# Alternating full and half-width experts, and wider weight blocks, in a mixture-of-experts layer

## The chip, the cores and the metric

The kernel runs on one core of a Trainium2 chip. The metric is device time in microseconds of one execution. Three executions of the kernel before gave 1993.58 us in the median (1984.93 to 1996.19). A separate execution was profiled; all rows below are from that one.

## The reference

Two transformer layers over 256 latent and 256 context tokens of width 1024, all in float32. The change concerns only the last step of the second layer, a mixture of eight experts of which each of the 256 latent tokens takes the best two:

```python
def moe_swiglu(h, w_router, wg, wu, wd):
    logits = t @ w_router
    top_v, top_i = lax.top_k(logits, 2)
    gates = ...            # softmax of the two, zero for the other experts
    for e in range(8):
        y = y + gates[:, e:e + 1] * ((silu(t @ wg[e]) * (t @ wu[e])) @ wd[e])
```

Each `wg[e]` and `wu[e]` is 1024 x 3584 and each `wd[e]` is 3584 x 1024, so an expert has 44.04 MB of weights and the eight have 352.3 MB. A token block is at most 128 rows, so every weight is used for few columns of work: weights have to stream in from HBM all through this step.

## The kernel before

The kernel runs the first layer, then the second layer's mixer, and ends with the experts, which take the second half of its time.

**Two kinds of expert.** The experts are sorted by how many tokens they got (`order_experts`, `order_index`), but for expert 0, which starts before the order is known. The first `NBIG` = 4 of them are *full*: up to 128 tokens each, handled by `expert`. The other four are *small*: up to 64 tokens, handled by `expert_small`. They run in the order 0 to 7, so all full ones come first. SP reads the order into registers in `load_order` (line 1049) and uses it in the addresses of all later weight loads. Tokens over these capacities would be handled in a loop at the end that is skipped where there are none.

**A full expert.** Weights come in loads of 1 MiB through `load_e`, each into a slot of a ring of 2048-column buffers (`slot32`; the names of the slots stand in `first` and `ring`, and `until` says up to which load a borrowed slot may be used: from load 62 on five slots are left). `convert` then splits each load in two float32r parts: ACT writes the high part `eh` (line 804), DVE subtracts to get the low part `el` (line 805). Three pairs of buffers hold converted weights. The product is made of three matmuls (high x high, high x low, low x high; `mm3`). The 3584 columns go in seven blocks of 512. For block j the order on the PE is: gate into PSUM tile `pg` (two loads, 24 matmuls of 512 columns), transposes of block j-1 (`g_T`), up into `pu` (the same again), `act_mul` (ACT: Silu of `pg`; DVE: times `pu`), and `down` of block j-1 into `pd` (two loads, 24 matmuls, line 1148). The last block's transposes and `down`, and the scatter of the result to the token rows (`scatter_pre`, `scatter_half`), are a *tail* that runs inside the first block of the next expert.

**A small expert.** The same loop without conversion: the loads are used as plain float32 (`load_raw`, line 1232), so a slot stays taken until the PE has read it. Gate and up go together into the two halves of the partitions of one PSUM tile `pgs` (line 1268); a matmul of 512 columns shows as two PE instructions, so that a block has 32 of them for gate and up, and 16 for down (`pds`, line 1256). The scatter writes `py` (line 1310).

**Loads.** All weight loads are issued by SP, in program order, one after the other; SP waits at each until its slot is free. A gate or up load takes 512 rows of 2048 contiguous bytes, a down load 256 rows of 4096 bytes. Loads that fit are issued before the experts begin: `prefetch` brings the first three while the mixer runs, and the slots of `first` are filled as soon as the mixer gives its memory back.

**Side work.** `plan` hangs small pieces of work on (expert, block): the ordering, the one-hot selections, the gathers of the token columns for later experts (`gather_at`, `gather_pair`, `gather_rest`), and broadcasts of vectors (`row_bc`).

## Time and profile before

| | |
|---|---|
| median of three executions | 1993.58 us |
| profiled execution | 1992.54 us |
| its span (first to last instruction) | 1990.6 us |
| mean granted TensorE clock | 0.979 |
| PE busy | 1851.6 us (93%) |
| DVE busy | 1000.7 us (50%) |
| ACT busy | 766.9 us (39%) |
| HBM read | 477.48 MB, 240 GB/s over the span |

PE is the engine for matmuls, DVE the vector engine, ACT the scalar engine, SP the engine that issues the loads. "Busy" sums the stretches in which an engine executed something; matmuls overlap in the pipeline, so a busy PE is not a PE at its peak. Shares over the whole span mix stages of different limits; the change touches the stage from 1006 us to the end.

### The profile page before, as it was taken

Reading aid. Unit: us, or ns where it says so; the run is one execution under the profiler, and the core shown is the slowest. Engines: PE = TensorE matmul, PEld = TensorE weight load, DVE = VectorE, ACT = ScalarE, POOL = GpSimd, SP = SyncE. Lnnn points to the kernel's source line nnn. Section 1 sums busy time; section 2 is a strip of 40 time slices with the busy share of each in tenths; the row PEclk is TensorE's granted clock in tenths of the full one; section 3 lists DMA queues with packets and bytes.
Section 4 is the critical chain, followed back from the end, with each engine's and each line's share of the span. In section 5 each row is a group of like instructions: output and inputs, shape, how many; then the busy total and the mean of one; then the engine's idle time right before and its main releaser. Section 6 shows DMA issues by size and latency. Waiting matters only on the chain.

```text
span 1990.6 us, 23382 instructions
## 1 busy us (share of the span) xinstructions
PE 1851.6 (93%) x9168; PEld 1275.5 (64%) x9168; DVE 1000.7 (50%) x1356; ACT 766.9 (39%) x991; POOL 49.1 (2%) x89
## 2 busy tenths in 40 slices
PE   7998999999999999999999999999999878887876
PEld 4866767778887877677677878878785322222222
DVE  5475665633333345756679788988984001010101
ACT  4324554422222234235566677767762000000001
POOL 1031000000000000200000000000000000000000
PEclk9999999999999999999989999999999999899998
DMA  9555242442344244553389688999998999999996
GB/s 326 178 166 144 69 142 71 138 137 69 101 130 157 78 127 151 141 141 127 124 300 361 243 325 312 342 350 365 348 339 289 390 394 388 377 390 386 388 385 258
DMA packets 287089, 480.13 MB, mean 241 GB/s; under 512 B 12206, under 2 KB 142636, under 8 KB 286972
## 3 DMA queue, kind: packets, MB, share of 16 engines
q1 hardware_dynamic: 283488, 474.32, 67.6%
q0 software_dynamic: 1232, 2.42, 1.0%
q10 hardware_dynamic: 2252, 1.83, 0.3%
q8 instruction: 74, 1.21, 0.3%
q14 instruction: 43, 0.35, 0.1%
HBM read 477.48 MB, written 1.05 MB: 240 GB/s over the span
## 4 chain that ended last, share of the span: by engine, by line
PE 78%; DMA 15%; DVE 4%; ACT 2%; issue 1%; SPq 0%; ACTq 0%; DVEq 0%
DMA e<-in_w_moe_up_dram 12%; PE pd L1148 8%; PE pgs L1268 6%; PE pds L1256 3%; PE pg L149 3%; PE pu L150 3%; PE pu L151 3%; PE pg L150 3%; PE pu L149 3%; PE pg L151 3%; PE psg L149 2%; PE psmod L229 2%; PE psg L150 2%; PE psg L151 2%; PE psu L149 2%; PE psp L149 2%
## 5 line engine op out<-in xcount | busy, mean ns | idle before, releaser
L805 DVE TENSOR_TENSOR el<-e,eh 128x2048 fp32r<-128x2048 f32 (+1 forms) x173 | 375.5, 2189 | 50.4 <-ACT eh L804 49.3
L804 ACT ACTIVATE eh<-e 128x2048 fp32r<-128x2048 f32 (+1 forms) x173 | 316.6, 1838 | 93.8 <-PE pd L1148 31.7
L1268 PE MATMUL pgs<-e,xs 128*64 128x512 f32 x896 | 247.6, 628 | 72.7 <-DMA e<-in_w_moe_up_dram 64.0
L1268 PEld LDWEIGHTS pgs<-e,xs 128*64 128x64 f32 x896 | 70.0, 142 | 235.0 <-DMA e<-in_w_moe_up_dram 105.7
L143 DVE TENSOR_TENSOR wl<-w,wh 128x2048 fp32r<-128x2048 f32 (+2 forms) x70 | 150.3, 2148 | 104.4 <-ACT wh L142 104.3
L142 ACT ACTIVATE wh<-w 128x2048 fp32r<-128x2048 f32 (+2 forms) x70 | 125.4, 1792 | 199.6 <-issue 78.3
L1277 DVE TENSOR_TENSOR eg<-eg,pgs 64x512 f32<-64x512 f32 x28 | 19.3, 690 | 360.7 <-ACT eg L1276 360.7
L1276 ACT ACTIVATE eg<-pgs 64x512 f32<-64x512 f32 x28 | 16.6, 591 | 374.1 <-PE pgs L1268 374.1
L1256 PE MATMUL pds<-e,gts 128*64 128x512 f32 x448 | 127.7, 599 | 0.2 <-DMA e<-in_w_moe_down_dram 0.2
L149 PE MATMUL psp<-hH,wh 128*128 128x512 f32 (+1 forms) x224 | 88.4, 397 | 3.4 <-ACT hH L274 3.3
L149 PE MATMUL pg<-eh,xeH 128*128 128x512 f32 x224 | 90.2, 403 | 0.6 <-ACT eh L804 0.6
L150 PE MATMUL pg<-el,xeH 128*128 128x512 f32 x224 | 89.9, 401 | 0.0
L151 PE MATMUL pg<-eh,xeL 128*128 128x512 f32 x224 | 89.2, 398 | 0.0
L149 PE MATMUL pu<-eh,xeH 128*128 128x512 f32 x224 | 89.0, 397 | 0.0
L150 PE MATMUL pu<-el,xeH 128*128 128x512 f32 x224 | 88.3, 394 | 0.7 <-DVE el L805 0.6
L149 PE MATMUL psq<-wh,hH 128*128 128x256 f32 x304 | 88.7, 292 | 0.0
L151 PE MATMUL psq<-wh,hL 128*128 128x256 f32 x304 | 88.2, 290 | 0.0
L150 PE MATMUL psq<-wl,hH 128*128 128x256 f32 x304 | 87.8, 289 | 0.0
L151 PE MATMUL pu<-eh,xeL 128*128 128x512 f32 x224 | 87.7, 392 | 0.0
L150 PE MATMUL psp<-hL,wh 128*128 128x512 f32 (+1 forms) x224 | 86.6, 387 | 0.0
L151 PE MATMUL psp<-hH,wl 128*128 128x512 f32 (+1 forms) x224 | 85.0, 380 | 0.0
L1148 PE MATMUL pd<-eh,gth 128*128 128x512 f32 x224 | 71.2, 399 | 2.7 <-ACT eh L804 2.5
(511 smaller groups left out, 3504.3 us busy)
## 6 DMA issues: line engine op xcount, KB each, us to landing
e<-in_w_moe_gate_dram SPq DMA_DIRECT2D x111, 1024.0 KB, 7.4
e<-in_w_moe_up_dram SPq DMA_DIRECT2D x111, 1024.0 KB, 7.7
e<-in_w_moe_down_dram SPq DMA_DIRECT2D x111, 1024.0 KB, 6.8
wmod<-in_w_mod_dram SPq DMA_DIRECT2D x96, 512.0 KB, 4.7
w<-in_w_in_dram SPq DMA_DIRECT2D x24, 1024.0 KB, 7.2
w<-in_w_ffn_gate_dram SPq DMA_DIRECT2D x11, 1024.0 KB, 7.5
w<-in_w_ffn_up_dram SPq DMA_DIRECT2D x11, 1024.0 KB, 5.2
w<-in_w_out_dram SPq DMA_DIRECT2D x8, 1024.0 KB, 5.2
```

The lines of the kernel that those rows point to most:

```text
L142: act(wh[:, :m], w32[:, :m], AF.Copy)
L143: tt(wl[:, :m], w32[:, :m], f32(wh[:, :m]), ALU.subtract)
L149: mm(ps, lhsT=sh, rhs=mh, start=first, stop=False)
L150: mm(ps, lhsT=sh, rhs=ml, start=False, stop=False)
L151: mm(ps, lhsT=sl, rhs=mh, start=False, stop=last)
L229: mm(ps[32 * k:32 * k + 32, :n], lhsT=Sz[:, k0 + k, :], rhs=wv[:, k, :], start=k0 == 0, stop=k0 == 4, skip_group_check=True)
L804: act(h3[:, b], w[:, b], AF.Copy)
L805: tt(l3[:, b], w[:, b], f32(h3[:, b]), ALU.subtract)
L1148: mm(pds[o], lhsT=gt[sh][:, q, :], rhs=w[mh][:, k, o * 512:(o + 1) * 512], start=a and j == 0 and q == 0, stop=z and j == NJ - 1 and q == 3)
L1256: mm(pd[0][H * o:H * o + H, :], lhsT=gt[:, q, :], rhs=w[:, k, o * 512:(o + 1) * 512], start=j == 0 and q == 0, stop=j == NJ - 1 and q == 3 ...
L1268: mm(ps[H * o:H * o + H, :], lhsT=xv[:, kk, :], rhs=ws[o][:, k, :], start=kk == 0, stop=kk == KD - 1, skip_group_check=True)
L1277: tt(g[0:H], g[0:H], ps[H:P], ALU.mult)
```

## The change

**Order.** The experts run as 0, 4, 1, 5, 2, 6, 3, 7: full and small ones alternate. `plan` is now keyed by place in that order and by half blocks (even keys run inside a block, odd ones behind it). The small experts' gather moves into the first full expert; the gathers for the full experts 1, 2 and 3 move into small ones.

**Blocks.** The 3584 columns go in four blocks of 896 (`FB`) instead of seven of 512. A gate or up load is 256 rows of 896 columns, 3584 contiguous bytes each and 0.92 MB in all; there are 32 per expert instead of 28. A down block of 896 rows is given to the partitions in sevens (row p*7+k goes to partition p), so a load of two k is 8192 contiguous bytes per partition; each block has three such loads of 1.05 MB and one of half that size, 16 per expert instead of 14.

**What follows from that.** Gate and up matmuls have 448 columns, two for each k in two PSUM banks; `pg` and `pu` are two banks wide and have one buffer instead of two. `act_mul` writes its result in permuted order (steps of 512 bytes within runs of seven) so that the transposes fit the new row order of down. `eg`, `gth` and `gtl` have one buffer instead of two.

**Ring.** The slot `xc` and its pieces of 1024 bytes are gone; 12 slots instead of 13 are filled first; `xl` stays in the ring to the end, so that six slots are left from load 42 on.

```diff
+FB = 896
+FK = FB // 128
...
+        m = kk * n
+        nc.sync.dma_start(w32[:, :m].rearrange("p (k n) -> p k n", n=n), dram)
+        for a in range(0, m, m // 2 if i < 8 else m):
+            b = slice(a, a + (m // 2 if i < 8 else m))
+            act(wh[:, b], w32[:, b], AF.Copy)
+            tt(wl[:, b], w32[:, b], f32(wh[:, b]), ALU.subtract)
...
+        ready[i] = convert(i, ring_tile(f"r{i}"), wm_g[0, 0, i * 256:(i + 1) * 256, 0:FB].rearrange("(k p) n -> p k n", p=P), 2, FB, mpr)
...
-    pgu = pool("pgu", 2, space=PSUM)
+    pgu = pool("pgu", 1, space=PSUM)
...
-    first = ["r0", "r1", "r2", "w", "c", "r0", "r1", "xh", "xl", "xt", "y", "r2", "xc"]
-    ring = ["w", "c", "r0", "r1", "xh", "xl", "xt", "y", "r2", "xc"]
-    until = {"xc": 36, "xt": 42, "y": 42, "xh": 62, "xl": 62}
+             "y": lambda: mp2.tile([P, 2048], F32, tag="y", name="e32")}
+    first = ["r0", "r1", "r2", "w", "c", "r0", "r1", "xh", "xl", "xt", "y", "r2"]
+    ring = ["w", "c", "r0", "r1", "xh", "xl", "xt", "y", "r2"]
+    until = {"xt": 42, "y": 42, "xh": 30}
...
-        xs = mp.tile([P, KD, n], F32, tag="xeH1", name="xs")
+        xs = mp.tile([P, KD, n], F32, tag="xeH0", name="xs")
...
+    NJ = FE // FB
+    HB = FB // 2
+
+    def gu_ap(w_ap, j, c):
+        return w_ap[c * 256:(c + 1) * 256, j * FB:(j + 1) * FB].rearrange("(k p) n -> p k n", p=P)
+
+    def down_aps(w_ap, j):
+        w = w_ap[j * FB:(j + 1) * FB, :].rearrange("(p k) n -> p k n", k=FK)
+        return [(k, min(2, FK - k), w[:, k:min(k + 2, FK), :]) for k in range(0, FK, 2)]
...
     def gate_up(w_ap, xe, j, tag):
...
+        ps = pgu.tile([P, 2, 512], F32, tag=tag, name=tag)
+        for c in range(KD // 2):
+            w = load_e(gu_ap(w_ap, j, c), 2, FB)
+            for k in range(2):
+                kk = 2 * c + k
+                for (sh, mh) in ((0, 0), (0, 1), (1, 0)):
+                    for b in range(2):
+                        mm(ps[:, b, 0:HB], lhsT=xe[sh][:, kk, :], rhs=w[mh][:, k, b * HB:(b + 1) * HB],
+                           start=kk == 0 and sh == mh, stop=kk == KD - 1 and sh == 1)
...
+    def by_row(ap):
+        return ap.rearrange("p h (q k) -> p h q k", k=FK)
+
+    def act_mul(g, pg, pu):
+        gv = g.rearrange("p (k h q) -> p h q k", h=2, q=P // 2)
+        act(gv, by_row(pg), AF.Silu)
+        tt(gv, gv, by_row(pu), ALU.mult)
+
+    def new_g():
+        return mp2.tile([P, FB], F32, tag="eg", name="eg")
 
...
+        gh = mp2.tile([P, FK, P], F32R, tag="gth", name="gth")
+        gl = mp2.tile([P, FK, P], F32R, tag="gtl", name="gtl")
+        for k0 in range(0, FK, 4):
+            n = min(4, FK - k0)
+            pt = bank(pmt, "pgt")
+            for q in range(n):
+                nc.tensor.transpose(pt[:, q * P:(q + 1) * P], g[:, (k0 + q) * P:(k0 + q + 1) * P], ident)
+            pv = pt[:, 0:n * P].rearrange("p (q n) -> p q n", n=P)
+            act(gh[:, k0:k0 + n], pv, AF.Copy)
+            tt(gl[:, k0:k0 + n], pv, f32(gh[:, k0:k0 + n]), ALU.subtract)
...
+        for q0, kn, ap in down_aps(w_ap, j):
+            w = load_e(ap, kn, D)
+            for k in range(kn):
+                q = q0 + k
...
-                           start=a and j == 0 and q == 0, stop=z and j == NJ - 1 and q == 3)
...
+                           start=a and j == 0 and q == 0, stop=z and j == NJ - 1 and q == FK - 1)
...
+            for f in (hooks or {}).get(2 * j, ()):
+                f()
             pu = gate_up(wu, xe, j, "pu")
-            g = act_mul(pg, pu)
+            g = new_g()
+            act_mul(g, pg[:, :, 0:HB], pu[:, :, 0:HB])
...
-            for f in (hooks or {}).get(j, ()):
+            for f in (hooks or {}).get(2 * j + 1, ()):
...
+            ps = pgu.tile([P, 2, 512], F32, tag=("pg", "pu")[j % 2], name="pgs")
+            for c in range(KD // 2):
+                ws = [load_raw(gu_ap(w_ap, j, c), 2, FB) for w_ap in (wg, wu)]
+                for k in range(2):
+                    kk = 2 * c + k
+                    for b in range(2):
+                        for o in range(2):
+                            mm(ps[H * o:H * o + H, b, 0:HB], lhsT=xv[:, kk, :], rhs=ws[o][:, k, b * HB:(b + 1) * HB],
...
+                if c == 1:
...
+            g = new_g()
+            act_mul(g[0:H], ps[0:H, :, 0:HB], ps[H:P, :, 0:HB])
...
-        xg = mp.tile([P, 2, D], F32, tag="xeH0", name="xg")
+        xg = mp.tile([P, 2, D], F32, tag="xeH1", name="xg")
...
-        xes[2] = gather_at(2, 2, xe_tiles(0))
+        xes[2] = gather_at(2, 2, xe_tiles(1))
...
-    plan = {(0, 1): [order_experts], (0, 2): [order_index, lambda: onehots(1, 1, posp)], (0, 4): [lambda: gather_at(1, 1, x01, P), load_order],
-            (0, 6): [lambda: row_bc(ga2b, lambda k: modT[1][:, 40 + k, 0:1])],
-            (1, 1): [lambda: onehots(2, 2, posp)], (1, 4): [gather_pair],
-            (2, 3): [add_x], (2, 5): [stack_ga2],
-            (3, 1): [onehots_twice], (3, 4): [gather_rest],
+    plan = {(0, 1): [order_experts], (0, 2): [order_index], (0, 3): [onehots_twice],
+            (0, 5): [gather_rest], (0, 6): [lambda: row_bc(ga2b, lambda k: modT[1][:, 40 + k, 0:1])], (0, 7): [load_order],
+            (1, 2): [lambda: onehots(1, 3, posp)], (1, 3): [add_x], (1, 5): [stack_ga2], (1, 6): [lambda: gather_at(1, 1, x01, P)],
+            (3, 4): [gather_pair],
             (4, 3): [lambda: row_bc(gfb, lambda k: gfT[:, k:k + 1])]}
...
-    for e in range(NE):
+    for i, e in enumerate([0, 4, 1, 5, 2, 6, 3, 7]):
```

## Rows read from the trace of the kernel before

**Rows 1.** The page, section 2: 40 slices of 49.8 us; DMA busy tenths, GB/s.

```profile
DMA  9555242442344244553389688999998999999996
GB/s 326 178 166 144 69 142 71 138 137 69 101 130 157 78 127 151 141 141 127 124 300 361 243 325 312 342 350 365 348 339 289 390 394 388 377 390 386 388 385 258
```

**Rows 2.** By tile, pg and pgs: ns min/median/max, first and last start (us).

```profile
L149 PE MATMUL pg<-eh,xeH x224: 387/396/735, 1006.1 to 1497.7; 128*128 128x512 f32 x112
...
L1268 PE MATMUL pgs<-e,xs x896: 592/592/1115, 1507.2 to 1965.1; 128*64 128x512 f32 x180
```

**Rows 3.** Windows: start:end, length, busy PE PEld DVE ACT POOL, granted clock, DMA share, GB/s.

```profile
1180.00:1300.00 120.00, 119.89 (x551) 97.45 (x550) 105.90 (x68) 86.17 (x59) 0.00 (x0) 1.00 0.89 324
1300.00:1400.00 100.00, 99.70 (x453) 80.68 (x452) 86.88 (x54) 70.75 (x46) 0.00 (x0) 1.00 1.00 358
1640.00:1760.00 120.00, 97.67 (x396) 31.34 (x391) 12.44 (x22) 5.50 (x11) 0.00 (x0) 0.96 1.02 384
1760.00:1870.00 110.00, 89.74 (x370) 28.84 (x372) 8.51 (x16) 5.68 (x11) 0.00 (x0) 0.98 1.03 389
```

**Rows 4.** Chain that ended last: start us, length us, engine, tile, line, count.

```profile
1197.10 5.55 PE pd L1148 x24
1214.15 5.55 PE pd L1148 x24
...
1645.79 1.72 PE py L1310 x4
...
1760.09 1.72 PE py L1310 x4
...
1972.28 1.96 PE pds L1256 x8
```

**Rows 5.** Windows of 3 us within the small experts.

```profile
1601.00:1604.00 3.00, 1.36 (x8) 0.30 (x6) 0.00 (x0) 0.00 (x0) 0.00 (x0) 1.00 1.05 408
...
1613.00:1616.00 3.00, 1.42 (x8) 0.56 (x10) 0.00 (x0) 0.00 (x0) 0.00 (x0) 1.00 1.04 385
```

**Rows 6.** Timeline of PE, output projection: start us, length us; 256 columns.

```profile
973.09 0.28 PE L151 MATMUL psw<-mH,wl 128*128 128x256 f32 x1
...
978.49 0.28 PE L151 MATMUL psw<-mH,wl 128*128 128x256 f32 x1
```

**Rows 7.** Timeline of PE, gate of a large expert; 512 columns.

```profile
1492.89 0.40 PE L149 MATMUL pg<-eh,xeH 128*128 128x512 f32 x1
...
1498.21 0.40 PE L151 MATMUL pg<-eh,xeL 128*128 128x512 f32 x1
```

**Rows 8.** Timeline of PE, gate and up of a small expert.

```profile
1940.05 3.78 PE L1268 MATMUL pgs<-e,xs 128*64 128x512 f32 x16 [1.73 <-DMA e<-in_w_moe_up_dram]
```

**Rows 9.** Windows where large experts end and small ones begin.

```profile
1510.00:1520.00 10.00, 10.00 (x44) 3.74 (x42) 1.18 (x3) 0.60 (x1) 0.00 (x0) 1.00 0.73 267
1520.00:1530.00 10.00, 5.93 (x15) 4.10 (x14) 5.18 (x3) 4.19 (x3) 0.00 (x0) 0.71 1.01 354
1530.00:1540.00 10.00, 10.00 (x37) 3.99 (x35) 4.73 (x7) 1.26 (x2) 0.00 (x0) 0.95 0.28 93
```

**Rows 10.** Timeline of the SP queue in that stretch.

```profile
1527.27 11.50 SPq L1232 DMA_DIRECT2D e<-in_w_moe_down_dram  x2
```

**Rows 11.** DVE groups, 1006 to 1140 us: count | busy us, mean ns.

```profile
L805 DVE TENSOR_TENSOR el<-e,eh 128x2048 fp32r<-128x2048 f32 x34 | 77.6, 2289 | 13.9 <-ACT eh L804 13.7
...
L1125 DVE TENSOR_TENSOR eg<-eg,pu 128x512 f32<-128x512 f32 x7 | 4.8, 680 | 0.0
...
L1036 DVE TENSOR_TENSOR pw<-perm,tab 128x64 f32<-128x64 f32 x1 | 0.3, 291 | 0.0
...
L1032 DVE TENSOR_TENSOR pw<-perm,tab 128x64 f32<-128x64 f32 x1 | 0.2, 218 | 0.0
```

**Rows 12.** Line 1049, the expert order read by SP.

```profile
L1049 SPq TENSOR_LOAD <-ordi x7: 261/262/487, 1056.2 to 1059.9; - x7
```

**Rows 13.** Chain that ended last, the gather of the first expert's tokens.

```profile
999.26 7.06 PE pga L1092 x32
```

More of the change, by code (lines that the diff above doesn't have):

```diff
@@ L1111, in gather_small @@
         return xs
-    def gate_up(w_ap, xe, j, tag):
-        ps = pgu.tile([P, 512], F32, tag=tag, name=tag)
-        for half in range(2):
-            w = load_e(w_ap[half * 512:(half + 1) * 512, j * 512:(j + 1) * 512].rearrange("(k p) n -> p k n", p=P), 4, 512)
-            for k in range(4):
-                mm3(ps, (xe[0][:, 4 * half + k, :], xe[1][:, 4 * half + k, :]), (w[0][:, k, :], w[1][:, k, :]),
-                    half == 0 and k == 0, half == 1 and k == 3)
-        return ps
-    def act_mul(pg, pu):
-        g = mp2.tile([P, 512], F32, tag="eg", name="eg", bufs=2)
-        act(g, pg, AF.Silu)
-        tt(g, g, pu, ALU.mult)
-        return g
@@ L1137, in g_T @@
         return gh, gl
-    NJ = FE // 512
     def down(w_ap, gt, j, pds):
-        for half in range(2):
-            w = load_e(w_ap[j * 512 + half * 256:j * 512 + (half + 1) * 256, :].rearrange("(k p) n -> p k n", p=P), 2, D)
-            for k in range(2):
-                q = 2 * half + k
+        for q0, kn, ap in down_aps(w_ap, j):
+            w = load_e(ap, kn, D)
+            for k in range(kn):
+                q = q0 + k
                 for (sh, mh, a, z) in ((0, 0, True, False), (0, 1, False, False), (1, 0, False, True)):
@@ L1184, in scatter_half, with expert @@
                 tt(xtk[:, t, cs], xtk[:, t, cs], py, ALU.add)
-    def expert(xe, wg, wu, wd, Sf, gate_col, tail, hooks=None, first=False, end=None):
+    def expert(xe, wg, wu, wd, Sf, gate_col, tail, hooks=None, first=False):
         pds = None
@@ L1211, in t1 @@
         def t1():
-            if end:
-                tc.keep_in_program_order(nc.scalar.preload_act_table_set(LN_EXP))
-                sc = scatter_pre(Sf, gate_col)
-                new_xg()
-                for o in range(2):
-                    down_cols(wd, last[0], pds, o)
-                    scatter_half(sc, pds, o)
-                    end(o)
-                return
             down(wd, last[0], NJ - 1, pds)
@@ L1241, in g_Ts @@
             pt = bank(pmt, "pgt")
-            for q in range(4):
+            for q in range(FK):
                 nc.tensor.transpose(pt[:, q * H:(q + 1) * H], g[0:H, q * P:(q + 1) * P], ident[0:H, 0:H])
-            gt = mp2.tile([P, 4, H], F32, tag="gth", name="gts", bufs=2)
-            copy_bal(gt, pt[:, 0:4 * H].rearrange("p (q n) -> p q n", n=H))
+            gt = mp2.tile([P, FK, H], F32, tag="gth", name="gts")
+            copy_bal(gt, pt[:, 0:FK * H].rearrange("p (q n) -> p q n", n=H))
             return gt
@@ L1274, in expert_small @@
                         tail[0]()
-            g = mp2.tile([P, 512], F32, tag="eg", name="eg", bufs=2)
-            act(g[0:H], ps[0:H], AF.Silu)
-            tt(g[0:H], g[0:H], ps[H:P], ALU.mult)
+                    for f in (hooks or {}).get(2 * j, ()):
+                        f()
+            g = new_g()
+            act_mul(g[0:H], ps[0:H, :, 0:HB], ps[H:P, :, 0:HB])
             if prev is not None:
@@ L1282, in expert_small @@
             prev = g
-            for f in (hooks or {}).get(j, ()):
+            for f in (hooks or {}).get(2 * j + 1, ()):
                 f()
```

65 lines of the change are left out of this document (14 added, 51 removed).

## The prediction

> **What bounds the kernel now.** I read the slices first, to find where the loads run near their limit [rows 1]: only in the second half, from about 1000 us, where the experts are. Then the tiles [rows 2]: the first gate matmul of expert 0 starts at 1006.1 us, the first matmul of a small expert at 1507.2. So the four full experts take 501.1 us, 125.3 each, and the rest, to the end at 1990.6, belongs to the small ones. The windows tell the two stages apart [rows 3]. With full experts PE is busy all the time and the loads move 324 to 358 GB/s. With small ones the loads move 384 to 389 GB/s at a share above 1.0, PE has gaps, and DVE and ACT are nearly idle. The chain says the same [rows 4]: a block of a full expert is 17.05 us (1214.15 - 1197.10), seven of them 119.4 us, 6 less than the 125.3; one small expert to the next is 114.30 us (1760.09 - 1645.79), that is 44.04 MB at 385 GB/s.
>
> So the full experts are bound by PE, by little: 44.04 MB in 119.4 us is 369 GB/s. The small ones are bound by the loads: 336 instructions per expert, 0.2125 us apart ((3.78 - 0.59)/15, [rows 2, 8]), are 71 us of PE, some 77 with transposes and scatter, against 114. The last load lands at 1972.3, 18.3 us before the end [rows 4].
>
> The loads cannot use the slack of the full stage for the small stage, since no more than five slots lie ahead. That is what the change is to be weighed by: from 1006.1 to 1972.3 the loads had 966 us; at 385 GB/s the 352.3 MB less 13.6 MB (the 13 slots filled before) take 880. Some 86 us of load time are unused.
>
> **The rate of the loads.** In the small stage a window of mostly 2048-byte runs moves 385 GB/s, the best one 408 [rows 5]; I read the latter as the 4096-byte runs of down, since a third of the time goes to these. With 16 engines that is 85.1 ns for a run of 2 KB and 160.6 for one of 4 KB: 9.6 ns fixed and 75.5 ns for each 2 KB. A run of 3584 bytes is then 141.7 ns (405 GB/s), one of 8192 is 311.6 ns (421). The mix before gives 392 by this (two thirds gate and up), the mix after 409 (six sevenths of down in long runs): 4.3% more. Scaled to the measured 385 it is 402 GB/s, 109.6 us per expert. Bounds: no gain, 385; no loss against the fit, 409. I take 402, as both ends of the fit are rows of the same stage.
>
> **PE in the full experts.** Matmuls of 256 columns start 0.120 us apart (5.40/45), of 512 columns 0.2313 us (5.32/23) [rows 6, 7]. On the line between, 448 columns take 0.2040. A new block has 96 of these (19.6), 42 of 512 columns (9.7) and seven transposes (1.75 times 17.05 - 72 x 0.2313 = 0.4, so 0.7): 30.0 us, against 1.75 x 17.05 = 29.8. Four blocks are 120 us, 0.6 more per expert. Small experts have the same columns; their PE time stays near 77.
>
> **Alternating.** In a pair of a full and a small expert PE has about 197 us of work plus side work (some 7 us for 32 gather matmuls with their copies [rows 13], a few such groups in all). The loads need 2 x 109.6 = 219.2. With the higher rate a full expert leaves 120 x 0.402 - 44.04 = 4.2 MB in hand, and six slots of 0.92 to 1.05 MB hold about 5.6. So the slack fits the ring, and the loads should run nearly without a break from the second expert on.
>
> First full expert: its loads begin with 12 slots (11 MB) in hand, so PE sets the time: 120, less the last down (9.7 us, moved to the next expert as before), plus 5 for side work (6 before, with the gather of the small tokens for a gather of the second expert's): 115, to 1121 us. By then the loads have brought 44.04 - 3.67 (last down) + 5.6 = 46.0 MB. Left are 306.3 MB, 762 us at 402 GB/s.
>
> Breaks of the loads: where a small expert follows a full one, its raw loads keep their slots while PE does the old expert's down and scatter. Before, this came once: in three windows the share was 0.73, 1.01, 0.28, a loss of 2.7 + 7.2 = 9.9 us, the granted clock fell to 0.71 in the middle one, and SP stood 11.5 us at two loads [rows 9, 10]. The sum of this page applied to the stage before (at 1507.2 left: 4 x 44.04 + 2.1 - 5.2 = 173.1 MB, 449.5 us at 385, 1956.7) falls 15.6 us short of 1972.3, so 15.6 is its upper price with five slots, 0 the lower. With six I take 7; four times 28. What is queued behind SP's wait is every later load; PE meanwhile has work in hand.
>
> End: the tail of 18.3 us stays, less 1 for a last load of half the size. Profiled time minus span is 1.9 us. Sum: 1121 + 762 + 28 + 17.3 + 1.9 = 1930. The profiled time before (1992.5) is 1 below the median shown, so no correction. That is 3.2% faster.
>
> **The rest of the edits.** Three tiles with one buffer instead of two: `pg` and `pu` must be read before the next block writes them, but 9.7 us of down lie between, against Silu and product of about 1 us each (680 ns for 512 columns, [rows 11], times 1.75); without that cover 2 us per block. The first block of an expert has no down of its own, but there the tail of the expert before stands. Conversion: 10.5 loads' worth per block x 2.29 = 24.0 us of DVE plus 2.4 for `act_mul` and `gtl` is 26.4 of 30.0: still covered. The order is read at the end of the first expert instead of its middle: seven reads from 1056.2 to 1059.9, under 4.3 us [rows 12], ahead of every later load in SP's queue, while the ring is full; without that cover 4 us. The gathers for full experts move from the PE-bound stage into the load-bound one, a gain of some us in places that the sum already counts as load-bound: nothing. 48 issues per expert for 42 are covered: SP mostly waits for slots.
>
> **The permuted `act_mul`.** It steps by 512 bytes in SBUF. The nearest rows are two products of 64 elements: 218 ns with plain operands, 291 with one operand read in steps of 32 bytes, 1.14 ns more for each element [rows 11]. For 896 elements read and written in steps that is 1 to 2 us on top of 1.2, so DVE reaches about 28.5 of 30.0 us per block: covered, if narrowly. The lower bound is no cost; the upper is open, as no row has a step of 512 bytes. The Trainium skill, page "SBUF — State Buffer", section "Specifications (TRN2)", says that full bandwidth needs at least two hits in a 16-byte line and that each access in a new line pays a penalty; this speaks against the new order, and the pair of rows agrees in sign. By the rule alone, which has no price, every element of the product would pay on both sides; by the rows, the sum stays as it is.
>
> **Rivals.**
> A, the forecast: 1930; its own range 1900 to 1955. Chance 0.47.
> B, the rate stays at 385: the speeds of 2 KB and 4 KB runs differ for another reason than their length. 306.3 MB take 796 us: 1964. For it: the three-microsecond windows are short; against: it is the only stretch over 400, and comes where down loads should be. 0.18.
> C, alternation gives nothing: converted buffers and slots are released too late in full experts, so that they stay at 125.3 us, and small ones take 109.6 each. Three full, four small, less about 5 us (the ring's 14 in hand, 9 for the last down): 1121 + 3 x 125.3 + 4 x 109.6 - 5 + 19 = 1949; up to 1977 with the breaks. For it: loads in full experts reached only 324 to 358 GB/s although slots were reused all the time. 0.12. Here also belongs that the change does not do what it says: the order is changed, but the ring is too short for it.
> D, no breaks and the rate of 409: 1121 + 749 + 19 = 1889. 0.08.
> E, `act_mul` breaks its cover. DVE becomes the bound from 4.8 us per product (30.0 - 24.0 - 1.2), four times the plain one; at 10 us PE waits 5 us per block, a full expert takes 140 us, 17 more than the 123 in which the loads still flow (44.04 + 5.6 MB at 402), and the end is 1930 + 20 + 3 x 17 = 2001. For it: DVE is at 88% already. 0.06.
> F, slower: the loads lose rate, as rows of one load now lie 14 and 28 KB apart from partition to partition, and half-size loads keep less in flight. From 306.3 / (1992 - 1121 - 28 - 19) = 372 GB/s down the kernel is slower than before; at 360 it is 2019. For it only that no row shows runs over 4 KB in a load of weights; against: the trend of the two lengths. 0.06. The remaining 0.03 lies beyond these, mostly slow.
>
> **Numbers.** The likeliest is A, 1930. A range of 1890 to 1975 leaves out E, F and a little of B, C and D. About 0.5%, 10 us, is what a measurement of this kernel can tell from no change: faster means below 1983. A, D, nearly all of B and C, and a little of E: 0.86; within: 0.06; slower: 0.08.
>
> **What the profile after would show.** Right: windows inside the experts all near 400 GB/s at a share of about 1.0, both in full and small ones; first full expert's end near 1121; gate matmuls 0.204 us apart; a pair in about 226 us. B shows as 385 at full share; C as windows near 350 in full experts with SP waiting for DVE's `el`; E as PE idle ended by DVE `eg` or `el`; F as full share under 372 GB/s. The forecast is wrong if the loads stand still more than 15 us at each change of expert, or if PE waits in full experts push the pair over 235 us.

## The result and the profile after

The changed kernel took 2010.49 us in the median (2006.31 to 2018.11) against 1993.28 for the kernel before on the same chip: 1.0088 times as long, 95% interval 1.0073 to 1.0103, so 0.9% slower. The forecast was 1930 us, with a range of 1890 to 1975. The profiled execution has a span of 2008.8 us and a mean granted clock of 0.975.

The page of the profile of the changed kernel ("after" from here on), section 2, against [rows 1]. The swing between the full half and the small half is gone, as alternating should do; but from 1155 us to the last slice but one the loads move 324 to 408 GB/s, where about 400 was forecast:

```profile
DMA  9555232342344244543469789999899999999896
GB/s 317 175 163 152 70 126 84 129 144 69 100 134 152 84 133 135 153 126 118 161 242 338 290 338 392 339 346 355 334 408 337 346 353 349 407 324 364 328 386 260
```

By tile, gate matmuls of full and of small experts (ns min/median/max, first and last start), against [rows 2]. Expert 0 starts at 1009.8 us, 3.7 later than before, and the first small expert at 1129.3, for a forecast of 1121:

```profile
L1126 PE MATMUL pg<-eh,xeH x256: 360/368/740, 1009.8 to 1849.7; 128*128 128x448 f32 x128
...
L1269 PE MATMUL pgs<-e,xs x1024: 539/539/591, 1129.3 to 1974.7; 128*64 128x448 f32 x171
```

Windows by expert (small, full, small, full, small, full; columns as in [rows 3]):

```profile
1129.00:1245.00 116.00, 103.50 (x488) 46.77 (x486) 26.76 (x32) 20.93 (x21) 0.00 (x0) 0.96 0.94 363
1245.00:1379.00 134.00, 128.81 (x576) 104.18 (x578) 100.81 (x60) 81.89 (x55) 0.00 (x0) 0.96 0.95 347
1379.00:1493.00 114.00, 98.56 (x462) 42.72 (x459) 25.57 (x27) 19.80 (x19) 0.00 (x0) 0.96 0.94 366
1493.00:1627.00 134.00, 128.15 (x596) 103.99 (x596) 101.72 (x62) 82.79 (x57) 0.00 (x0) 0.99 0.95 347
1627.00:1742.00 115.00, 93.73 (x430) 38.43 (x426) 22.83 (x23) 18.71 (x15) 0.00 (x0) 0.96 0.95 371
1742.00:1872.00 130.00, 124.51 (x576) 100.66 (x574) 100.60 (x60) 80.70 (x54) 0.00 (x0) 1.00 0.96 351
```

A pair of a small and a full expert takes 249.5, 247.8 and 245.5 us, 247.6 in the mean, where 226 were forecast; before, 125.3 and 114.3 made 239.6. Three pairs are 65 us of the 80 that the forecast missed, the later end of the first expert 8, the rest lies in the last small expert and the tail.

Where the loads are not held up, they are as fast as forecast. Three windows of after, against [rows 5]:

```profile
1430.00:1440.00 10.00, 8.95 (x47) 4.55 (x48) 2.02 (x4) 1.20 (x2) 0.00 (x0) 1.00 1.02 405
1450.00:1460.00 10.00, 7.98 (x43) 3.26 (x41) 1.66 (x1) 1.72 (x1) 0.00 (x0) 1.00 1.01 421
1460.00:1470.00 10.00, 9.56 (x38) 2.92 (x34) 0.00 (x0) 0.54 (x1) 0.00 (x0) 0.83 1.03 404
```

But they are held up at each change from full to small. The timeline of the SP queue at the first change, against [rows 10]: no load between 1155.77 and 1165.15, since the slots hold raw weights that PE does not read while it does the old expert's down and scatter:

```profile
1153.42 0.37 SPq L1233 DMA_DIRECT2D e<-in_w_moe_gate_dram  x1
1155.77 0.37 SPq L1233 DMA_DIRECT2D e<-in_w_moe_up_dram  x1
1165.15 0.37 SPq L1233 DMA_DIRECT2D e<-in_w_moe_gate_dram  x1
```

The timeline of PE and of ACT there (the brackets: idle time before, and what ended it). Down of the old expert waits for conversions (`eh`) that stand on ACT behind the small expert's Silu (`eg`), and on DVE behind its product; its first matmuls then start about 0.43 us apart, from 1153 on 0.23 (the granted clock is 0.80 from 1149 to 1159, 1.00 behind it):

```profile
1143.44 0.50 PE L1169 MATMUL pst<-gates,S 128*128 128x1 f32 x4
1146.71 1.22 PE L1161 MATMUL pd<-eh,gth 128*128 128x512 f32 x2 [2.77 <-ACT eh L797]
1149.04 1.22 PE L1161 MATMUL pd<-el,gth 128*128 128x512 f32 x2 [1.10 <-DVE el L798]
1150.06 1.05 PE L1161 MATMUL pd<-eh,gtl 128*128 128x512 f32 x2
...
1154.16 0.62 PE L1161 MATMUL pd<-eh,gtl 128*128 128x512 f32 x2
```

```profile
1143.27 1.68 ACT L1135 ACTIVATE eg<-pgs 64x896 f32<-64x896 f32 x1 [6.10 <-PE pgs L1269]
1144.76 5.49 ACT L797 ACTIVATE eh<-e 128x2048 fp32r<-128x2048 f32 x3
```

The other thing to see is the product of a block. Silu (ACT) and product (DVE) of `act_mul` in after, by tile (ns min/median/max), full and small:

```profile
L1135 ACT ACTIVATE eg<-pg x16: 1792/1836/1848, 1024.5 to 1850.9; 128x896 f32<-128x896 f32 x16
L1136 DVE TENSOR_TENSOR eg<-eg,pu x16: 1728/1810/1832, 1033.3 to 1861.2; 128x896 f32<-128x896 f32 x16
L1135 ACT ACTIVATE eg<-pgs x16: 1670/1714/1730, 1143.3 to 1975.3; 64x896 f32<-64x896 f32 x16
L1136 DVE TENSOR_TENSOR eg<-eg,pgs x16: 1662/1664/1712, 1145.0 to 1977.1; 64x896 f32<-64x896 f32 x16
```

The product at 1.81 us is below the 2.2 to 3.2 that the prediction worked out from [rows 11]. That Silu is stretched too was not in the sum.

### The profile page after: what moved, and what is told of

It is laid out like the page before. It is cut to its first block, busy times and chain, and to the rows that moved or that the text cites. A ratio compares the mean times of both kernels' runs of the same rounds, so it can differ in the third digit from the quotient of the medians.

```text
span 2008.8 us, 24183 instructions
## 1 busy us (share of the span) xinstructions
PE 1864.1 (93%) x9488; PEld 1325.3 (66%) x9488; DVE 1020.7 (51%) x1353; ACT 791.3 (39%) x989; POOL 49.2 (2%) x89
## 3 DMA queue, kind: packets, MB, share of 16 engines
HBM read 477.48 MB, written 1.05 MB: 238 GB/s over the span
## 4 chain that ended last, share of the span: by engine, by line
PE 73%; DMA 9%; DVE 9%; ACT 5%; issue 4%; SPq 0%; ACTq 0%; DVEq 0%
PE pgs L1269 8%; DMA e<-in_w_moe_up_dram 6%; PE pd L1161 6%; PE pg L1126 5%; DVE el L798 4%; PE pu L1126 4%; PE pds L1257 4%; ACT eh L797 2%; PE psg L151 2%; PE psmod L231 2%; PE psg L152 2%; PE psp L151 2%; PE psg L153 2%; PE psu L151 2%; PE psu L152 2%
## 5 line engine op out<-in xcount | busy, mean ns | idle before, releaser
L798 DVE TENSOR_TENSOR el<-e,eh 128x1792 fp32r<-128x1792 f32 (+2 forms) x200 | 382.6, 1947 | 68.7 <-ACT eh L797 68.3
L797 ACT ACTIVATE eh<-e 128x1792 fp32r<-128x1792 f32 (+2 forms) x200 | 324.5, 1643 | 163.2 <-PE pd L1161 54.5
L1269 PE MATMUL pgs<-e,xs 128*64 128x448 f32 x1024 | 221.5, 545 | 27.1 <-DMA e<-in_w_moe_up_dram 26.2
L1135 ACT ACTIVATE eg<-pgs 64x896 f32<-64x896 f32 x16 | 27.3, 1707 | 222.1 <-PE pgs L1269 222.1
L1161 PE MATMUL pd<-el,gth 128*128 128x512 f32 x224 | 76.1, 422 | 9.0 <-DVE el L798 9.0
L1126 PE MATMUL pg<-el,xeH 128*128 128x448 f32 x256 | 77.3, 384 | 7.0 <-DVE el L798 6.3
L1126 PE MATMUL pg<-eh,xeH 128*128 128x448 f32 x256 | 76.5, 381 | 0.4 <-ACT eh L797 0.3
L1126 PE MATMUL pu<-el,xeH 128*128 128x448 f32 x256 | 74.9, 374 | 1.5 <-DVE el L798 0.4
L1126 PE MATMUL pg<-eh,xeL 128*128 128x448 f32 x256 | 75.1, 375 | 0.0
L1257 PEld LDWEIGHTS pds<-e,gts 128*64 128x64 f32 x448 | 34.5, 142 | 60.2 <-issue 56.2
```

The lines of the kernel that those rows point to most:

```text
L797: act(wh[:, b], w32[:, b], AF.Copy)
L798: tt(wl[:, b], w32[:, b], f32(wh[:, b]), ALU.subtract)
L1126: mm(ps[:, b, 0:HB], lhsT=xe[sh][:, kk, :], rhs=w[mh][:, k, b * HB:(b + 1) * HB], start=kk == 0 and sh == mh, stop=kk == KD - 1 and sh == 1)
L1161: mm(pds[o], lhsT=gt[sh][:, q, :], rhs=w[mh][:, k, o * 512:(o + 1) * 512], start=a and j == 0 and q == 0, stop=z and j == NJ - 1 and q == ...
L1257: mm(pd[0][H * o:H * o + H, :], lhsT=gt[:, q, :], rhs=w[:, k, o * 512:(o + 1) * 512], start=j == 0 and q == 0, stop=j == NJ - 1 and q == F ...
L1269: mm(ps[H * o:H * o + H, b, 0:HB], lhsT=xv[:, kk, :], rhs=ws[o][:, k, b * HB:(b + 1) * HB], start=kk == 0, stop=kk == KD - 1, skip_group_c ...
```

## The experiments

Each ran in three or five rounds beside the kernel before on its chip (1992.7 to 1994.6 us there). The first four set theory Q (the instructions stand in the wrong place at the changes of expert) against theory K (the large blocks cost it).

**1. The order alone**, blocks of 512 as before:

```diff
-    for e in range(NE):
+    for i, e in enumerate([0, 4, 1, 5, 2, 6, 3, 7]):
```

> The kernel before with its seven blocks of 512 and its loads, only the order of the experts is changed to full, small, full, small; the side work and the borrowed slots are moved as far as the order needs it (five to six slots are left, as in the changed kernel). Theory Q (the loss sits at the changes of kind: in-order queues of ACT and DVE hold the next expert's conversions behind the old expert's tail or the new one's product, PE stands and its clock falls; seven such changes instead of one): slower than before, 2000 to 2025 us, with PE gaps in the first block of every expert. Theory K (the loss sits inside the blocks: steps of 512 bytes in the product, 448 columns, shorter loads): the order alone is a gain, 1960 to 1985 us.

1992.78 us, ratio 1.0004 (0.9986 to 1.0022): no change, between the two. The full experts behind the first stay at 124 to 128 us; the first small one takes 109.5, the second and third 120.5 and 121.2, where before one small expert to the next took 114.3. I read this as: what alternating gives, the three added changes from full to small take; the run does not separate the two. It also has one slot more than the kernel before from load 62 on, since `xl` is not needed for tokens in this order. The windows of its second full and second small expert:

```profile
1236.00:1361.10 125.10, 121.80 (x518) 94.22 (x518) 101.30 (x58) 81.06 (x52) 0.00 (x0) 0.97 1.01 366
1361.10:1481.60 120.50, 105.64 (x440) 41.38 (x439) 20.85 (x31) 15.05 (x20) 0.00 (x0) 0.96 0.94 351
```

**2. The blocks alone**: the changed kernel in the order 0 to 7, with the gathers at their old places. With these, `xl` leaves the ring, so that five slots are left from load 70 on; the kernel before has five as well, the changed kernel six.

```diff
-    until = {"xt": 42, "y": 42, "xh": 30}
+    until = {"xt": 42, "y": 42, "xh": 70, "xl": 70}
...
-    for i, e in enumerate([0, 4, 1, 5, 2, 6, 3, 7]):
+    for i, e in enumerate(range(NE)):
```

> The changed kernel with its blocks of 896 and its loads, but with the experts in the old order 0 to 7 and the side work on its old places. Theory Q: small experts become bound by loads of about 410 GB/s, 108 us instead of 114, full ones cost some 4 us more (31.5 instead of 29.8 us per block): 1975 to 1992 us. Theory K: 2000 to 2020 us, full experts well over 130 us each.

2015.92 us, ratio 1.0117 (1.0095 to 1.0140). So the loss is in the blocks: K. A full expert (the third) took 6 us more than the 125.3 before, a small one (the second) 3.5 less than 114.3, at the higher rate:

```profile
1262.10:1393.40 131.30, 127.74 (x618) 110.34 (x618) 114.47 (x76) 91.66 (x63) 0.00 (x0) 1.00 0.93 335
1649.50:1760.30 110.80, 90.85 (x413) 32.26 (x410) 11.76 (x13) 7.95 (x6) 0.00 (x0) 0.95 1.00 394
```

**3 and 4. The tails.** In the first block of a small expert the old expert's down with its conversions (`tail[1]`) comes ahead of Silu and product, which are held in program order, and its scatter (`tail[2]`) behind them; in 4 also the small expert's scatter goes into the second block of the next full one:

```diff
+            if prev is None and tail:
+                tail[1]()
             g = new_g()
-            act_mul(g[0:H], ps[0:H, :, 0:HB], ps[H:P, :, 0:HB])
+            act_mul(g[0:H], ps[0:H, :, 0:HB], ps[H:P, :, 0:HB], prev is None)
...
             elif tail:
-                tail[1]()
+                tail[2]()
```

> The changed kernel; in the first block of a small expert the ACT and DVE queues take the conversions of the old full expert's last down ahead of the Silu and the product, and the scatter comes behind these. Theory Q: PE's gap of about 4 us and the slow matmuls behind it go at four places, 15 to 30 us less: 1980 to 1995 us. Theory K: within 5 us of the changed kernel's 2010.

> As the run before, and in the first blocks of a full expert the scatter of the old small expert is queued on DVE behind the conversions of the next gate block instead of ahead of them. Theory Q: a further 8 to 10 us less at each of three places: 1950 to 1975 us. Theory K: within 5 us of 2010.

2008.32 us, ratio 1.0078 (1.0050 to 1.0106), and 2005.91, ratio 1.0062 (1.0038 to 1.0086): theory K in both. The medians are 2 and 5 us below the changed kernel's 2010.49, but the intervals overlap with its 1.0073 to 1.0103, so that no gain by Q is shown here.

**5. The plain product.** Silu and product read and write in plain order; the rest is as in after, so the columns of the product no longer belong to the rows of down that they meet.

```diff
-        gv = g.rearrange("p (k h q) -> p h q k", h=2, q=P // 2)
-        act(gv, by_row(pg), AF.Silu)
-        tt(gv, gv, by_row(pu), ALU.mult)
+        gv = g.rearrange("p (h n) -> p h n", h=2)
+        act(gv, pg, AF.Silu)
+        tt(gv, gv, pu, ALU.mult)
```

> The changed kernel with one edit: Silu and product of a block read and write their 896 columns in plain order, while the down rows are still loaded in runs of 8192 bytes. The columns of the product then no longer belong to the down rows that they are multiplied with; no work is left out. Theory S (the permuted product costs the time): the changed kernel's trace has Silu and product at 1.7 to 1.8 us each, plain ones of 896 columns would be near 1.1 (590 and 690 ns per 512 columns before); in small experts PE stands about 1.6 us per block between the down and the transposes for it, so 16 x 0.6 to 1.2 us there and some tenths in each of the 16 full blocks: 1988 to 2000 us. Theory N (it is covered, the 20 us are elsewhere in the large blocks): 2003 to 2012.

1990.07 us, ratio 0.9980 (0.9963 to 0.9998): theory S. The 20 us go with the permuted product.

**6 and 7. One slot less, one slot more.** In 6 `xl` leaves the ring at load 62; in 7 a seventh slot is added, for which `eg` moves onto a table that is dead by then.

```diff
-    until = {"xt": 42, "y": 42, "xh": 30}
+    until = {"xt": 42, "y": 42, "xh": 30, "xl": 62}
...
-    ring = ["w", "c", "r0", "r1", "xh", "xl", "xt", "y", "r2"]
+    ring = ["w", "w2", "c", "r0", "r1", "xh", "xl", "xt", "y", "r2"]
```

> The changed kernel with one slot of the ring fewer from load 62 on: five instead of six. Theory R (the number of slots bounds the loads: each slot is 0.92 to 1.05 MB, 2.3 to 2.6 us of the loads at every change from full to small, and a shorter queue in the full blocks): 3 or 4 changes x 2.5 us plus 1 to 2 us in each of 12 full blocks, 2025 to 2045 us. Theory N (the slots hold enough, PE's own work and the place of the instructions set the time): within 5 us of 2010.

> The changed kernel with a seventh slot of 8 KB per partition in the ring (the buffer of the product is moved onto the table of the attention, that is no longer used then). Theory R (the number of slots bounds the loads): 1990 to 2002 us, the loads' breaks at the changes shorter by about 2.5 us each and fewer waits of PE in full blocks. Theory N: within 4 us of 2010.

2040.46 us, ratio 1.0252 (1.0217 to 1.0287), and 2005.70, ratio 1.0072 (1.0047 to 1.0096). Downward R holds (30 us); upward the median is 5 us lower, just outside N and farther from R, with an interval that overlaps that of after.

**8. Interleaved by blocks.** From the second full expert on, two streams of blocks of 512 take turns.

```diff
+    full, small = stream(range(NBIG)), stream(range(NBIG, NE))
+    for _ in range(NJ):
+        next(full)
+    for _ in itertools.zip_longest(full, small):
+        pass
```

> Blocks of 512 and loads as in the kernel before, but from the second full expert on, full and small experts alternate block by block: one block of a full expert, one of a small one, and so on for 21 blocks each; the last 7 small blocks stand alone. A pair of blocks has 17 + 11 us of PE and 12.6 MB, 32.7 us at 385 GB/s. Theory R (the idea of sharing the slack is right, but the slots hold only a few us of loads, so that it has to be shared within a block and not over an expert of 120 us): loads near 385 GB/s all the way from 1126 us, 306 MB in 796 us, end near 1940, 1930 to 1960 us. Theory C (the loads lose their rate whenever full blocks convert beside them, so 350 to 360 GB/s): 1975 to 2000. Theory N (PE has to wait for converts and scatters at every change of block): above 2000.

2004.33 us, ratio 1.0060 (1.0040 to 1.0081): N, and unexpected. Two pairs of blocks that I followed took 34.7 and 34.5 us, not 32.7; the mean of the twenty from 1133.9 to 1832.1 us is 34.9. In the first of the two PE waits, at its change to the full block, for the low part of the first weights. From 1200 to 1900 us the weight loads of such matmuls wait 35 us in all for DVE's `el`, in 20 places. I take it that six slots do not let these weights be loaded and converted much ahead; no run gives this order more slots:

```profile
1554.43 0.50 PE L150 MATMUL pg<-eh,xeH 128*128 128x512 f32 x1
1557.22 0.50 PE L151 MATMUL pg<-el,xeH 128*128 128x512 f32 x1 [2.29 <-DVE el L807]
```

C falls as the main cause: in windows of 5 us with converts going on (1554 to 1574) the loads moved 387 to 405 GB/s.

**9 and 10. Two ways to a plain product.** In 9 the transposes read every seventh column instead; in 10 down is loaded in runs of 4096 bytes as before and nothing is permuted.

```diff
+    def rows_k(g, k):
+        return g.rearrange("p (q k) -> p k q", k=FK)[:, k]
...
-                nc.tensor.transpose(pt[:, q * P:(q + 1) * P], g[:, (k0 + q) * P:(k0 + q + 1) * P], ident)
+                nc.tensor.transpose(pt[:, q * P:(q + 1) * P], rows_k(g, k0 + q), ident)
```

```diff
-        w = w_ap[j * FB:(j + 1) * FB, :].rearrange("(p k) n -> p k n", k=FK)
+        w = w_ap[j * FB:(j + 1) * FB, :].rearrange("(k p) n -> p k n", p=P)
```

> The changed kernel with the permutation moved from the product to the PE: Silu and product of a block read and write plain, and the seven transposes of a block read every seventh column of the product (28 bytes apart) in place of 128 that lie together. Loads of down keep their runs of 8192 bytes. Theory S (the permuted Silu and product cost the 20 us that the plain order took away): 1986 to 1996 us, about the 1990 of the run with the plain order, if the transposes take no longer than the 109 ns (full) and 64 ns (small) apart that they are now. Theory T (the steps cost as much wherever they are read): transposes of a full expert several hundred ns each, 2000 to 2015.

> The changed kernel with no permutation at all: rows of down are dealt to the partitions as in the kernel before, in runs of 4096 bytes, and Silu and product are plain. By the fit of the prediction 117 MB of down at 408 in place of 421 GB/s are 9 us, half of it in stretches that the loads bound. Theory L (the long runs bring what the fit says): 4 to 8 us above the run with strided transposes, 1993 to 2000. Theory M (runs over 4 KB bring nothing that counts): within 2 us of it.

1990.66 us, ratio 0.9985 (0.9972 to 0.9999), and 1993.84, ratio 0.9993 (0.9978 to 1.0008). Theory S again. The long runs of down are worth some 3 us, between L and M, and the intervals overlap. Rows of run 9 against those of after above (full, then small):

```profile
L1135 ACT ACTIVATE eg<-pg x16: 913/924/927, 1026.3 to 1833.6; 128x896 f32<-128x896 f32 x16
L1136 DVE TENSOR_TENSOR eg<-eg,pu x16: 1079/1087/1089, 1034.4 to 1843.5; 128x896 f32<-128x896 f32 x16
L1135 ACT ACTIVATE eg<-pgs x16: 911/911/911, 1143.1 to 1957.5; 64x896 f32<-64x896 f32 x16
L1136 DVE TENSOR_TENSOR eg<-eg,pgs x16: 1089/1089/1090, 1144.4 to 1958.5; 64x896 f32<-64x896 f32 x16
```

The pair takes 2.0 us instead of 3.6 (full) and 3.4 (small). Who waits for it, first in after, then in run 9 (us, times):

```profile
  PEld pgt L1244: 31.4, 12
  PE pgt L1244: 20.9, 12
```

```profile
  PEld pgt L1244: 15.6, 12
  PE pgt L1244: 5.0, 12
```

In 12 of the 16 small blocks PE stands until the product is there, 1.3 us longer in after: 16 us in all. Only part of this is time of the kernel, as the small experts wait for loads too: as a whole a small one is 1.6 us shorter in run 9 than in after, a full one 4.5 (table in the next section). In full blocks the two keep ACT and DVE from converting. Waits of a steady stretch with full blocks (after, 1315.6 to 1378.8; us, times, longest):

```profile
PEld pd L1161 <- DVE el L798: 1.1, 2, 0.6
PEld pg L1126 <- DVE el L798: 1.0, 2, 0.5
PEld pu L1126 <- DVE el L798: 1.0, 2, 0.5
```

In run 9 only the second of these rows is left (1308.4 to 1369.9), and a steady block takes 30.7 us instead of 31.6.

**11, 13 and 14. Slot and tails without the permuted product; 18. with it.** All on run 9 but 18, which is on after.

> The run with strided transposes, and added to it a seventh slot (2005.7 us alone in the changed kernel, 5 less) and the two tails moved as before (2005.9 alone, 4 less). Theory R (slots and the place of the tails count by themselves, whatever the product costs): 1978 to 1985 us, faster than both kernels. Theory N (they only covered part of the product's cost, which is gone): 1986 to 1994.

> The run with strided transposes (1990.7) and the seventh slot alone, without the moved tails. Theory R (the slots are what the loads lack at the changes of expert): 1968 to 1978 us, most of the 28 us. Theory A (each part brings what it brought in the changed kernel, and the rest is the two together): 1984 to 1988.

> The run with strided transposes (1990.7) and the two moved tails alone, with six slots. Theory R: 1982 to 1988 us. Theory P (PE's stand at the change is what holds the slots; once conversions come ahead of the waiting product, the loads flow): 1966 to 1976.

> The changed kernel as it is, permuted Silu and product included, with the seventh slot and the moved tails. Theory S (the permuted pair costs PE its wait in each block, whatever the loads do): 1979 to 1987 us, 17 to 24 above the 1962.5 with strided transposes. Theory H (loads that flow hide it): 1963 to 1972.

| us, median | six slots | seventh slot | tails moved | both |
|---|---|---|---|---|
| permuted product (after) | 2010.5 | 2005.7 | 2005.9 | 1990.3 |
| strided transposes (run 9) | 1990.7 | 1984.8 | 1990.4 | **1962.5** |

Run 11 is faster than both kernels, the one before by 1.5%: 0.9846 (0.9828 to 0.9863). The slot alone brings 6 us (theory A of run 13), the tails alone nothing (neither theory of run 14), both together 28, so that the time lies below what either theory of run 11 gave. The permuted product costs 28 us once the two are there: theory H of run 18 falls, and its 1990 lie above S. A window of 10 us from about 30 us after the fourth change to a small expert shows it: after, run 9, run 13 (slot), run 14 (tails), run 11 (both), in this order:

```profile
1902.00:1912.00 10.00, 10.00 (x42) 3.90 (x42) 5.42 (x8) 1.26 (x2) 0.00 (x0) 1.00 0.44 154
```

```profile
1884.00:1894.00 10.00, 10.00 (x43) 3.62 (x42) 5.42 (x8) 1.26 (x2) 0.00 (x0) 1.00 0.52 172
```

```profile
1878.00:1888.00 10.00, 10.00 (x43) 3.61 (x42) 5.42 (x8) 1.26 (x2) 0.00 (x0) 1.00 0.54 185
```

```profile
1880.00:1890.00 10.00, 10.00 (x42) 3.54 (x41) 5.43 (x8) 1.26 (x2) 0.00 (x0) 1.00 0.52 184
```

```profile
1860.00:1870.00 10.00, 10.00 (x51) 4.07 (x52) 1.42 (x3) 0.54 (x1) 0.00 (x0) 1.00 1.03 417
```

Here the break of the loads stays with either one and is gone with both; at the first change it is nearly gone in run 13 too, with the slot alone. Why neither is enough alone at the later changes I have not settled.

**12. The blocks with strided transposes in the old order.**

> The blocks of 896 with strided transposes, in the old order of the experts (0 to 7). With the permuted product this order took 2015.9 us, 5.4 more than the alternating one. Theory S: 20 us less, 1992 to 2000. If alternating is worth nothing by itself (blocks of 512: 1992.8 against 1993.3), this run is within 4 us of the run with strided transposes; if large blocks make it worth something (the higher rate leaves more slack), 5 to 15 us above it.

2001.51 us, ratio 1.0047 (1.0025 to 1.0069): 14 us below run 2, a little short of theory S, and 11 us above run 9. But as in run 2 the old order has five slots from load 70 on, where run 9 has six, and in the changed kernel that one slot was worth 30 us (run 6). So the 11 us are order and slot together; no run has both orders with large blocks and equal slots, but for runs 2 and 6 with five each, where the alternating one is 25 us slower.

**15. Nine slots** from the middle of expert 5, the fourth in order, on; run 11 is the base.

```diff
     def gather_pair():
         xes[2] = gather_at(2, 2, xe_tiles(1))
+        ring.extend(["hH", "hL"])
```

> The run with seven slots, tails and strided transposes (1962.5), and from the middle of the fourth expert on two more slots, nine in all, on the place of the tokens that have been gathered for the last time then. For this the path for experts with more tokens than their share, which is not run on these inputs, is cut to its last lines. Theory R (the forecast's sum needs more slots): the pairs after 1470 us fall from 233.5 us to about 222 to 228, the end comes at 1940 to 1952 us. Theory N (seven are enough, the rest is PE's own time: 30.7 us per block and what stands around the first one): 1956 to 1966.

1951.37 us, ratio 0.9802 (0.9762 to 0.9843): theory R by the median; the interval still touches that of run 11, so that the trace has to decide. The only small expert that is followed by a full one behind that point, and the two together:

```profile
1598.80:1697.00 98.20, 90.48 (x432) 38.52 (x431) 21.32 (x25) 15.03 (x15) 0.00 (x0) 1.00 1.00 398
1697.00:1825.10 128.10, 124.85 (x576) 102.87 (x576) 97.72 (x59) 78.69 (x54) 0.00 (x0) 0.99 1.00 384
sum 226.30, PE 215.33 PEld 141.39 DVE 119.04 ACT 93.72 POOL 0.00; mean PE 107.67 PEld 70.69 DVE 59.52 ACT 46.86 POOL 0.00
```

The same pair in run 11, with seven slots, sums to 230.90, so two more slots bring 4.6 us here, all in the small expert. The loads run at full share almost throughout: only the last 50 us of the full expert fall to 343 to 360 GB/s.

**16 and 17. Slot and tails with blocks of 512**, alternating and in the old order.

> Blocks of 512 with loads in runs of 2 and 4 KB in the alternating order (1992.8 us), with the same seventh slot and moved tails. Theory L (longer runs are 4% more rate, which the load-bound half turns into time): 1972 to 1985 us, 10 to 20 above the 1962.5 of the large blocks. Theory M (slots and tails are all of it): 1958 to 1967.

> The kernel before (order 0 to 7, blocks of 512) with the seventh slot and the moved tails, nothing else. Theory A (alternating shares the slack of the full experts as soon as the slots carry it over the change): this order has no slack to share in the small half, so only its one change and the small tails gain, 1983 to 1991 us, 14 or more above the 1969.5 of the same in alternating order. Theory B (slots and tails gain by themselves, alternating gives nothing): 1966 to 1974.

1969.51 us, ratio 0.9876 (0.9841 to 0.9911), and 1991.88, ratio 0.9992 (0.9971 to 1.0012). Theory A, if just beyond its upper end: the old order gains nothing from slot and tails, the alternating one 23 us. One reserve: in the old order `xl` leaves the ring at load 62, so that the added slot makes six there and seven in run 16; what a seventh would do in the old order was not run. With the large blocks and their strided transposes the same is 7 us faster (run 11), between L and M, but the intervals overlap.

## Why the prediction was wrong

Mean times of a pair of small and full expert (three pairs each; for run 15 the one shown):

| us | forecast | after | run 9 | run 18 | run 11 | run 15 |
|---|---|---|---|---|---|---|
| small | 106 | 115.2 | 113.6 | 108.0 | 104.9 | 98.2 |
| full | 120 | 132.4 | 127.9 | 134.4 | 127.4 | 128.1 |
| pair | 226 | 247.6 | 241.5 | 242.4 | 232.3 | 226.3 |

The pair of after took 21.6 us more than forecast, 12.4 in the full expert (4.5 of these go with the permuted product, the rest is PE's time for its blocks) and 9.2 in the small one. By way of run 9, 6 us go with the permuted product and 9 with the missing slot and the place of the tails; by way of run 18 it is 5 for slot and tails and 10 for the product, so the shares depend on the order. Two more slots bring 5 to 6. That run 15 then stands at the 226 of the forecast is chance: the forecast had 120 + 106 with a break of 7 us in it, the run has 128 + 98 and hardly a break.

- **The stock of the ring** is the step that failed. By the prediction a full expert leaves 4.2 MB in hand, six slots hold 5.6, "so the slack fits the ring, and the loads should run nearly without a break". What a small expert finds loaded, less what it leaves loaded for the next one, is its 44.04 MB less what moved in its own window (GB/s times length): 1.9 MB in the three windows of after, in the mean, and 1.9 in the last one of run 9, both with six slots, 3.0 in run 11 with seven, 5.0 in run 15 with nine. The rows of run 9 and run 11, against those of after and run 15 above:

```profile
1614.40:1727.30 112.90, 94.73 (x431) 40.26 (x430) 21.27 (x24) 15.02 (x15) 0.00 (x0) 0.97 0.95 373
1599.70:1704.00 104.30, 91.16 (x432) 38.39 (x431) 21.21 (x25) 14.96 (x15) 0.00 (x0) 1.00 1.00 393
```

 By that some four slots are tied up in keeping the loads going, and only those beyond them carry anything over, about 1 MB each. The 2.3 MB that lack in after are 5.7 us at 402 GB/s. The slack was larger, too: a full expert of 132.4 us could have left 132.4 x 0.402 - 44.04 = 9.2 MB. Why it is four I only argue. By the page of after a load takes 7 to 8 us from issue to landing (last column), and 402 GB/s x 7.5 us are 3 MB, more than three slots, to which one in conversion or being read is to be added. But this time is no constant: for gate loads it is 6.9 us with five slots (run 6) and 10.2 with seven (run 11), so it seems to hold some waiting behind loads issued before.

```profile
e<-in_w_moe_gate_dram SPq DMA_DIRECT2D x128, 896.0 KB, 7.4
e<-in_w_moe_up_dram SPq DMA_DIRECT2D x128, 896.0 KB, 7.6
e<-in_w_moe_down_dram SPq DMA_DIRECT2D x96, 1024.0 KB, 8.2
```

 This is rival C, in the form "the order is changed, but the ring is too short for it": windows near 350 in full experts, and SP waiting for DVE's `el` (406 us in 175 places from 1009 to 1990 us), as it said. Its 1949 to 1977 were too low: it left the full expert at 125.3 and the small one at 109.6.
- **The permuted product**: its size on DVE was put too high rather than too low (1.81 us for 2.2 to 3.2), but "covered, if narrowly" was wrong, and that Silu on ACT is stretched as well was left out. Per block ACT and DVE lose 0.9 + 0.7 us (full). The cover was checked by adding up DVE's busy time of a block, 28.5 of 30; but PE waits for the last of a chain, PSUM to ACT to DVE to transposes, which no busy sum shows. For the small experts nothing was asked, as DVE is nearly idle there; yet PE stands still for it there, 1.3 us per block. Of the 20 us that run 9 gives back, about 15 still lie in the full experts. Rival E waited for 4.8 us per product; 1.8 were enough. The Trainium skill, page "SBUF — State Buffer", section "Specifications (TRN2)", says that each access that crosses to a new 16-byte line pays a penalty; the rows above agree in sign and give the price of steps of 512 bytes here, 1.0 ns per element for Silu and 0.8 for the product.
- **A full block of 30.0 us**: 31.6 measured in the steady part, 30.7 without the permuted product. The matmuls were right: of 448 columns, 24 in 4.92 us (1840.47 to 1845.39), 0.205 apart for 0.204 (the line through its two rows gives 0.2035). Half a us of the 0.7 left in run 9 is the wait for `el` that its steady blocks still show (1.0 us in two blocks); the rest was not traced. First blocks take 33 to 37 us with the tail of the expert before them, second ones 32 to 36, and the sum had 30 for each in the three full experts that follow a small one. In run 9 these two blocks cost 5 us per full expert over steady ones of 30.7. The kernel before had 6 over its steady blocks (125.3 against 119.4), and the sum kept such a term for the first expert only.
- **The breaks at the changes**: sized nearly right. At the fourth change the window of 154 GB/s lacks (405 - 154)/405 x 10 = 6 us, for 7 in the sum. A whole small expert, its time less what moved in it at 402 GB/s, loses 10 us in after, 9 in run 9, 3 in run 11 and 1 in run 15.
- **The rate of the loads**: right, 404 to 421 GB/s where nothing holds the loads up, and also beside conversions (410 in run 15 from 1737 to 1757 us), so rivals B and F fall. Runs 10 and 16 say that it is worth a few us as long as slots and PE set the time, within the noise.
- **The single-buffered tiles, the order read later, the moved gathers**: no wait in the rows above names them; they were not tried by themselves. The 3 to 4 us of a later start lie before the experts and were left open; the runs with the changed start scatter between 1005.0 and 1011.6.

The pair of 247.6 us is past the 235 at which the prediction had said that it would be wrong.

## What to carry to other kernels

A ring of buffers carries slack over a change of stage only with the slots beyond those that the transfers in flight and the reader tie up, here two of six. Measure it: the gain of a stage from the stock is its need less what moves in its own window. An operation with little busy time can still set the pace when it sits in a chain between engines: ask who waits at its end in every stage, and for which other engines it is stretched as well. A layout that makes transfers longer at the cost of a strided access can be paid on the engine that reads anyway in small pieces: here the transposes took it for nothing that could be seen in the time, and the longer runs themselves brought no more than 3 us. And remedies may need each other: changes whose medians fall by 20, 5 and 5 us one at a time on the changed kernel bring 48 together (2010.5 to 1962.5).

## What the runs showed of the hardware that was not expected

- Writing in steps of 512 bytes nearly doubles a Silu on ACT (1836 against 924 ns for 128 x 896); reading one operand and writing in such steps stretches a product on DVE by two thirds (1810 against 1087).
- A transposing matmul that reads columns 28 bytes apart has a weight load of 212 ns instead of 140 (medians); the kernel's time did not show it. By tile, after and then run 9:

```profile
L1148 PEld LDWEIGHTS pgt<-ident,eg x112: 137/140/143, 1041.6 to 1868.1; 128*128 128x128 f32 x112
```

```profile
L1148 PEld LDWEIGHTS pgt<-ident,eg x112: 197/212/224, 1042.9 to 1849.9; 128*128 128x128 f32 x112
```

- From issue to landing a gate load of 0.92 MB took 6.9 us in the median with five slots in the ring (run 6), 7.4 with six (after) and 10.2 with seven (run 11).
